# First norm of a streaming encoder layer: shared load buffers, small loads on GpSimd's queue, another order of the modulation steps

## The chip, the cores and the metric

The kernel runs on one core of a Trainium2 chip, as one program. The metric is the device time of a run in microseconds. The kernel before took 885.54, 887.25 and 888.99 us in three runs, median 887.25 us. TensorE is written PE, VectorE DVE, ScalarE ACT, GpSimd POOL and SyncE SP; SP issues nearly all of the DMAs here.

## The reference

One layer of a streaming encoder, 512 prompt tokens and 64 sample tokens, width 1024. Only its beginning matters for the change:

```python
def residual_block(x, c, mixer, w_ada, b_ada, norm1_g, w_out, norm2_g, w_ff1, w_ff2):
    sh1, sc1, g1, sh2, sc2, g2 = ada_modulation(c, w_ada, b_ada)   # silu(c) @ w_ada + b_ada, in six parts
    h = rms_norm(x, norm1_g) * (1 + sc1) + sh1
    ...
    # mixer(h): h @ w_in, split into q, k, v, qi, ki, wi, ga, gb;
    # sparse attention on the first six, a causal convolution on ga * sigmoid(gb);
    # then the output projection, a second modulated norm, a squared-ReLU MLP, a final norm
```

## The kernel before, in words

The two matrices `w_ada` and `w_in` come from HBM while the norm is computed, so the beginning is a race between loads and arithmetic. "The front" here means all up to the first matmul of the projection of `qi` (line L288), which starts 58.26 us into the profiled span. What follows it (projection, attention, convolution, MLP) is the same in both kernels.

- **Loads (L125 to L185).** SP issues them in program order: the conditioning rows `crow`, five token tiles `xtok0` to `xtok4` (L135) with six small loads into `rows` between them (biases and gains, L139), then `w_ada` in five blocks. A block (`BLOCKS`, `load_block`, L143 to L153) holds the shift and the scale columns for two (blocks 0 to 2) or one (blocks 3, 4) of the eight 128-wide slices of the width; it is four DMAs into tiles tagged `ada`, of which there are 10. Between the blocks come three slices of `w_in` (`load_w`): `ki`, `gb0`, `ga0`, and six small loads into `small` (convolution weights and state, L177 to L179). POOL's queue holds no DMA.
- **Constants (L189 to L207).** POOL makes the index matrix `jp`, `ones`, `onec`, `eps` and zeroes `cs`; DVE makes the identity from `jp`. ACT's first instruction that needs one of them reads `eps`.
- **Norm (L255 to L272).** For each token tile ACT squares and sums (L259), takes the root (L260), DVE scales, PE transposes against the identity (L270), ACT and DVE copy into `hat`. `columns` (L210) turns `crow` and `rows` and gives `cs` = silu(c) (L214).
- **Modulation step of a block (`mod_steps`, L225 to L249).** 16 matmuls on PE (L232, 32 rows in the trace: a plain f32 matmul shows two rows), ACT copies the result into `modrow`, PE turns it with `sel` (L239), DVE adds the biases and forms the scale (L246, L249).
- **Slices (`modulate`, L276).** For slice k, ACT writes the rounded high half of `h` (L281), DVE the full value (L282) and the low half (`sub`, L113).
- **Weights (`first_w`, L383).** ACT writes the high half of a weight slice, another engine the low half (L113): POOL for `ki` and `gb0`, DVE for `ga0`. They are called `fw0`, `fw1`, `fw2` in the trace's names, high and low half `fw00`, `fw01` and so on.
- **Products (`products(k, m, ...)`, L397).** For slice k and weight m, six matmuls at L406 of 288 columns each: high times high, low weight times high, high weight times low, for two halves of the tokens. There are 8 x 3 = 24 products, written (k, m) below, and they add up in six banks.

The orders of PE, ACT and DVE are written out by hand (the `manual_schedule` from L188, and the calls from `next(fr[0])` on to `step(...)`): what is called first is issued first on each of the three. In a `step`, a number b takes the next part of block b (first its matmuls, then the rest of the step with the first slice, then the second slice), and a tuple is products. POOL and SP take their instructions in the order of the program. An engine issues in order, so an instruction that waits holds up all that stand behind it.

Of the kernel before, what the change touches and what calls it, by code (L numbers as in the profile page):

```python
# [7 lines left out]
FT = mybir.dt.float32  # L8
# [7 lines left out]
D = 1024  # L16
# [13 lines left out]
TOPS = 256  # L30
FF = 4096
W = 31
ADA = 10
VEC, PEC = (0, 3), (1, 2)

P = dict(PRW=30, TPE=5, CS0=43, KYW=5, TAP=2, T0=20, IDX=2, TKS=12, ATT=4, SMP=6, MOD=21, CPW=15, MODL=6, S0=4, KEYW=5, TAPW=8, SCW=14, MODW=20, QIW=6, CSW=16, TKW=9, TK2=2, TKP=2, ATW=6, SMW=6, TT=3, CN1=8, CN2=21, CN3=8, RT=3, CNW=17)
HALO = W - 1
# [32 lines left out]
def step_kernel(ctx: ExitStack, tc: tile.TileContext, io):  # L70
    nc = tc.nc
    act, dve, pool, pe = nc.scalar, nc.vector, nc.gpsimd, nc.tensor

    def new_pool(stack, name, bufs=1):
        return stack.enter_context(tc.tile_pool(name=name, bufs=bufs, reuse_waits="tile"))
# [11 lines left out]
    def bank(tag, bufs):  # L87
        return ps.tile([128, 512], FT, name="ps_" + tag, tag=tag, bufs=bufs)

    def p_acc():  # L90
        return bank("acc", 3)

    def p_lg():
        return bank("lg", 2)

    def p_tp():
        return bank("tp", 2)

    def p_av():
        return bank("av", 1)  # L100
# [18 lines left out]
    def xtile(i):  # L119
        return (x_p[128 * i:128 * i + 128], 128) if i < 4 else (x_s, SAMP)  # L120

    start = ExitStack()
    stp = new_pool(start, "start")

    rows = stp.tile([128, 128], FT, name="rows")  # L125
# [5 lines left out]
    xt = []  # L131
    for i in range(5):
        src, n = xtile(i)
        t = stp.tile([128, D], FT, name=f"xtok{i}")
        nc.sync.dma_start(t[:n], src)  # L135
        xt.append((t, n))
        for r, ap in parts[2 * i:2 * i + 2]:
            k = ap.shape[1] // 128
            nc.sync.dma_start(rows[r:r + k, :], ap.rearrange("o (n c) -> (o n) c", c=128))  # L139

    BLOCKS = ((0, 2), (2, 2), (4, 2), (6, 1), (7, 1))

    def load_block(b):  # L143
        f0, nf = BLOCKS[b]
        tiles = []
        for v in range(2):
            for kh in range(2):
                t = stp.tile([128, 4, 256], FT, name="ada", tag="ada", bufs=ADA)[:, :, :128 * nf]
                c0 = 1024 * v + 128 * f0
                nc.sync.dma_start(t, w_ada[512 * kh:512 * kh + 512, c0:c0 + 128 * nf].rearrange("(k p) c -> p k c", p=128))  # L150
                tiles.append(t)
        return tiles
# [3 lines left out]
    def load_w(name, src, r0, c0, n=128):  # L156
        raw = wgt.tile([128, NK, 128], FT, name="wraw", tag="wraw", bufs=3)
        nc.sync.dma_start(raw[:, :, :n], src[r0:r0 + 1024, c0:c0 + n].rearrange("(k p) c -> p k c", p=128))
        wraw[name] = (raw, n)

    def split_w(name, hi=None, lo=None, eng=pool):
        raw, n = wraw.pop(name)
        if hi is None:
            hi = wgt.tile([128, NK, 128], FR, name="whi", tag="whi", bufs=2)
            lo = wgt.tile([128, NK, 128], FR, name="wlo", tag="wlo", bufs=2)
        copy_to(act, hi[:, :, :n], raw[:, :, :n])
        sub(eng, lo[:, :, :n], raw[:, :, :n], f(hi[:, :, :n]))
        return hi, lo, n

    small = stp.tile([128, 2, 512], FT, name="small")  # L170
    pool.memset(small[:, 0], 0.0)
    pool.memset(small[:64, 1], 0.0)
    ada = [load_block(0)]
    load_w("ki", w_in, 0, C_KI, 72)
    for s in range(4):
        n = 8 if s < 3 else 7
        nc.sync.dma_start(small[32 * s:32 * s + n, 0], io["conv_w"][0][s:s + 4 * n - 3:4])  # L177
    nc.sync.dma_start(small[:W, 1], io["conv_w"][0])
    nc.sync.dma_start(small[32:32 + HALO, 1], io["state_conv"][0, 0])  # L179
    load_w("gb0", w_in, 0, C_GB)  # L180
    ada.append(load_block(1))
    load_w("ga0", w_in, 0, C_GA)
    for b in (2, 3, 4):
        ada.append(load_block(b))


    begin = ExitStack()
# [3 lines left out]
    ones = cst.tile([128, 128], FT, name="ones")  # L191
# [117 lines left out]
    def fetch():  # L309
        if order:  # L310
            raw = wgt.tile([128, 1024], FT, name="wraw", tag="wraw", bufs=3)
            src = order.pop(0)
            nc.sync.dma_start(raw.rearrange("p (k c) -> p k c", k=src.shape[1]), src)
            raws.append(raw)

    def split():
        if raws:
            raw = raws.pop(0)
            hi = wgt.tile([128, 1024], FR, name="whi", tag="whi", bufs=2)
            lo = wgt.tile([128, 1024], FR, name="wlo", tag="wlo", bufs=2)  # L320
            for c in (slice(0, 512), slice(512, 1024)):
                copy_to(act, hi[:, c], raw[:, c])
                behind[0] = pool.tensor_tensor(lo[:, c], raw[:, c], f(hi[:, c]), op=OP.subtract).ins  # L323
            ready.append((hi, lo))
# [58 lines left out]
    def first_w(m, eng):  # L383
        hl = [stp.tile([128, NK, 128], FR, name=f"fw{m}{z}") for z in range(2)]
        fw[m] = split_w(("ki", "gb0", "ga0")[m], *hl, eng=eng)
# [11 lines left out]
    def products(k, *ms):  # L397
        h = hT[k]
        for i in ((0, 1), (2,)):
            for m in ms:  # L400
                hi, lo, n = fw[m]
                for j in range(2):
                    t = banks[2 * m + j][:n, :HALF]
                    for z in i:
                        w, x = ((hi, 0), (lo, 0), (hi, 1))[z]
                        pe.matmul(t, lhsT=w[:, k, :n], rhs=h[:, x, JS[j]], start=k + z == 0, stop=k == NK - 1 and z == 2)  # L406
# [36 lines left out]
    def step(*todo):  # L443
        if not banks:
            banks.extend([p_acc(), p_acc(), p_acc(), p_lg(), p_lg(), p_av()])
        for e in todo:
            if isinstance(e, int):
                next(fr[e])
            else:
                products(*e)  # L450

    next(fr[0])
    first_w(0, pool)
    next(fr[0])
    setup = conv_setup()
    next(setup)
    first_w(1, pool)
    step((0, 0), 0)
    next(setup, None)
    step((1, 0), (0, 1))  # L460
    first_w(2, dve)
    step(1, (1, 1), 1, 1, (0, 2), (1, 2), (2, 0, 1, 2), (3, 0))
    step(2, (3, 1), 2, 3, 2, (3, 2), 3, (4, 0, 1, 2))
    fetch()
    fetch()
    ckr = big.tile([128, 8, 2, 64], FT, name="ckr", tag="b")
    for s in range(2):
        nc.sync.dma_start(ckr[:, :, s, :], io["cache_kidx"][0, 0].rearrange("(n p) d -> p n d", p=128))
    step(4, (5, 0), 4)
    split()  # L470
    step((5, 1), (5, 2), (6, 0), (7, 0))
    for j in range(2):
        evac_ki(j, banks[j][:, :HALF], JS[j])
    step((6, 1), (7, 1), (6, 2), (7, 2))
# [898 lines left out]
```

## Time and profile before

| what | value |
|---|---|
| runs | 885.54, 887.25, 888.99 us |
| profiled execution | 887.81 us, its span 885.8 us |
| mean granted clock of PE | 0.963 of full speed |
| busy share of the span | PE 92%, DVE 58%, ACT 45%, POOL 33% |
| DMA | 95.55 MB, 107 GB/s of HBM over the span |
| first L288 matmul | 58.26 us into the span |

All times below are in microseconds from the span's start in the profiled execution. The page's row for PE reads `4898997977988999...` in 40 slices of some 22 us each: the first slice, 40% busy, and a part of the second and third are the front. The page's row for DMA reads `8984165...`: the first three slices are nearly full of transfers. The page's chain of waits covers the later part only, so the front is read from the timelines of the engines.

### The profile page before, as it was taken

To read this page: it belongs to the slowest core of one execution; us is meant where nothing else is said; L and a number is where in the kernel's file an instruction comes from. 1 tells how busy PE (TensorE), PEld (TensorE's weight loads), DVE (VectorE), ACT (ScalarE), POOL (GpSimd) and SP (SyncE) were. 2 spreads that over 40 slices of the span, in tenths; PEclk is the share of its full clock that TensorE was granted. 3 is DMA by queue.
4 is the path that set the end of the run, shared out by engine and by line. 5 is a ranking of instruction groups with operands and counts; after the bars stand their busy time and mean duration, and the time that the engine had idled before them with its cause. 6 is when DMAs were issued, how large, how long until landed. Compare 5 with 4: busy or idle time off the path is not lost. (4 is left out here: it accounts for less than half of the span.)

```text
span 885.8 us, 17048 instructions
## 1 busy us (share of the span) xinstructions
PE 815.4 (92%) x6787; PEld 758.7 (86%) x6787; DVE 509.6 (58%) x1133; ACT 402.0 (45%) x897; POOL 294.9 (33%) x273
## 2 busy tenths in 40 slices
PE   4898997977988999999899899998999989999996
PEld 3697894657877888989899899997999989999995
DVE  3579879999996344645856412663126631266343
ACT  5365554555876787554454211442124421244322
POOL 1155423122435323232423243332433333333700
PEclk9799998989999999999999899998999989999999
DMA  8984165445434356542312223222232223222411
GB/s 233 302 219 122 36 179 131 118 97 145 114 94 120 100 153 177 161 120 72 90 41 85 72 72 90 79 72 72 72 96 73 72 72 87 81 72 72 143 61 47
DMA packets 164553, 95.55 MB, mean 108 GB/s; under 512 B 7699, under 2 KB 161119, under 8 KB 164475
## 3 DMA queue, kind: packets, MB, share of 16 engines
q1 hardware_dynamic: 164475, 94.48, 38.3%
q8 instruction: 53, 0.87, 0.4%
q14 instruction: 25, 0.20, 0.1%
HBM read 88.82 MB, written 5.64 MB: 107 GB/s over the span
## 5 line engine op out<-in xcount | busy, mean ns | idle before, releaser
L113 POOL TENSOR_TENSOR wlo<-wraw,whi 128x1024 fp32r<-128x1024 f32 x52 | 125.0, 2403 | 239.0 <-ACT whi L104 230.0
L288 PE MATMUL ps_acc<-h,whi 128*128 128x288 f32 (+1 forms) x608 | 190.2, 313 | 0.0
L289 PE MATMUL ps_acc<-h,whi 128*128 128x288 f32 (+1 forms) x608 | 181.2, 298 | 0.0
L290 PE MATMUL ps_acc<-h,wlo 128*128 128x288 f32 (+1 forms) x608 | 180.8, 297 | 0.0
L104 ACT ACTIVATE whi<-wraw 128x512 fp32r<-128x512 f32 (+1 forms) x112 | 90.6, 823 | 151.4 <-PE ps_acc L289 49.0
L323 POOL TENSOR_TENSOR wlo<-wraw,whi 128x512 fp32r<-128x512 f32 x60 | 80.0, 1349 | 159.3 <-ACT whi L104 159.0
L288 PEld LDWEIGHTS ps_acc<-h,whi 128*128 128x128 f32 x608 | 115.9, 191 | 14.0 <-issue 12.7
L289 PEld LDWEIGHTS ps_acc<-h,whi 128*128 128x128 f32 x608 | 116.1, 191 | 0.9
L290 PEld LDWEIGHTS ps_acc<-h,wlo 128*128 128x128 f32 x608 | 116.0, 191 | 0.0
L1246 DVE TENSOR_TENSOR z<-z 128x288 f32<-128x288 f32 x64 | 79.3, 1242 | 43.4 <-ACT z L1245 43.4
L1078 DVE SCALAR_TENSOR_TENSOR x<-ps_acc,mod,x 128x288 f32<-128x288 f32 (+4 forms) x90 | 35.8, 422 | 95.5 <-PE ps_acc L290 95.3
L104 ACT ACTIVATE a<-z 128x288 fp32r<-128x288 f32 x64 | 28.2, 443 | 79.4 <-DVE z L1246 79.4
L555 DVE SCALAR_TENSOR_TENSOR yc<-u,cw,yc 128x606 f32<-128x606 f32 x60 | 58.6, 984 | 0.6
L1245 ACT ACTIVATE z<-z,bs 128x64 f32<-128x64 f32 (+2 forms) x96 | 39.9, 449 | 34.4 <-DVE z L1242 34.3
L113 DVE TENSOR_TENSOR a<-z,a 128x288 fp32r<-128x288 f32 x64 | 35.4, 556 | 29.7 <-ACT a L104 28.7
L738 ACT ACTIVATE gc<-sful,sg 128x544 bf16<-128x544 f32 x48 | 35.8, 746 | 32.1 <-DVE sg L736 31.3
L288 PE MATMUL ps_acc<-a,whi 128*128 128x288 f32 x168 | 49.9, 297 | 0.0
L290 PE MATMUL ps_acc<-a,wlo 128*128 128x288 f32 x168 | 49.9, 297 | 0.0
L289 PE MATMUL ps_acc<-a,whi 128*128 128x288 f32 x168 | 49.8, 297 | 0.0
L289 PE MATMUL ps_lg<-h,whi 128*128 128x290 f32 (+1 forms) x160 | 47.4, 296 | 0.0
L290 PE MATMUL ps_lg<-h,wlo 128*128 128x290 f32 (+1 forms) x160 | 47.3, 296 | 0.0
L288 PE MATMUL ps_lg<-h,whi 128*128 128x290 f32 (+1 forms) x160 | 47.2, 295 | 0.0
(359 smaller groups left out, 2110.1 us busy)
## 6 DMA issues: line engine op xcount, KB each, us to landing
wraw<-w_ff SPq DMA_DIRECT2D x64, 512.0 KB
ada<-w_ada SPq DMA_DIRECT2D x44, 512.0 KB
wraw<-w_in SPq DMA_DIRECT2D x24, 512.0 KB
wraw<-w_out SPq DMA_DIRECT2D x8, 512.0 KB
rep<-ud SPq DMA_DIRECT2D x24, 115.0 KB
xtok<-x_prompt SPq DMA_DIRECT2D x4, 512.0 KB
ada<-w_ada SPq DMA_DIRECT2D x8, 256.0 KB
ct<-cache_k SPq DMA_DIRECT2D x8, 256.0 KB
```

Of the source, the lines that this page charges most:

```text
L104: act.activation(out, in_, AF.Copy, scale=1.0 if scale is None else scale)
L113: eng.tensor_tensor(out, a, b, op=OP.subtract)
L288: pe.matmul(out, lhsT=hi, rhs=src[:, 0, cs_], start=first, stop=False)
L289: pe.matmul(out, lhsT=hi, rhs=src[:, 1, cs_], start=False, stop=False)
L290: pe.matmul(out, lhsT=lo, rhs=src[:, 0, cs_], start=False, stop=last)
L323: behind[0] = pool.tensor_tensor(lo[:, c], raw[:, c], f(hi[:, c]), op=OP.subtract).ins
L555: dve.scalar_tensor_tensor(yc[c], src, w, yc[c], op0=OP.mult, op1=OP.add)
L738: act.activation(eq, sful, AF.Sign, bias=cands[:, z:z + 1], scale=-1.0, accum_out=cnts[:, z:z + 1])
L1078: dve.scalar_tensor_tensor(xm[:, a:b], t[:, a - r.start:b - r.start], mod[:, g, s, m:m + 1], xm[:, a:b], op0=OP.mult, op1=OP.add)
L1245: act.activation(q, q, AF.Relu, bias=bs[:, s:s + 1])
L1246: dve.tensor_tensor(z[:, 1, r], z[:, 0, r], z[:, 0, r], op=OP.mult)
```

## The change

`ADA` goes from 10 to 15 and the five token tiles take their buffers under the same tag, so that later blocks may reuse a token tile's buffer. The six loads into `rows` and the six into `small` are issued by POOL instead of SP, the latter behind the loads of the blocks in program order. The low halves of `ki` and `gb0` are computed by DVE instead of POOL. A new function `warm(n)` issues n matmuls of `ones` by `ones` on PE whose result nobody reads. The order of modulation steps and products is another.

```diff
-ADA = 10
+ADA = 15
...
-        t = stp.tile([128, D], FT, name=f"xtok{i}")
+        t = stp.tile([128, D], FT, name=f"xtok{i}", tag="ada", bufs=ADA)
...
-            nc.sync.dma_start(rows[r:r + k, :], ap.rearrange("o (n c) -> (o n) c", c=128))
+            pool.dma_start(rows[r:r + k, :], ap.rearrange("o (n c) -> (o n) c", c=128))
...
-    for s in range(4):
-        n = 8 if s < 3 else 7
-        nc.sync.dma_start(small[32 * s:32 * s + n, 0], io["conv_w"][0][s:s + 4 * n - 3:4])
-    nc.sync.dma_start(small[:W, 1], io["conv_w"][0])
-    nc.sync.dma_start(small[32:32 + HALO, 1], io["state_conv"][0, 0])
     load_w("gb0", w_in, 0, C_GB)
     ada.append(load_block(1))
     load_w("ga0", w_in, 0, C_GA)
     for b in (2, 3, 4):
         ada.append(load_block(b))
+    for s in range(4):
+        n = 8 if s < 3 else 7
+        pool.dma_start(small[32 * s:32 * s + n, 0], io["conv_w"][0][s:s + 4 * n - 3:4])
+    pool.dma_start(small[:W, 1], io["conv_w"][0])
+    pool.dma_start(small[32:32 + HALO, 1], io["state_conv"][0, 0])
...
+    def warm(n):
+
+        t = p_tp()
+        for _ in range(n):
+            pe.matmul(t[:, :128], lhsT=ones, rhs=ones, start=True, stop=True)
+
+    first_w(0, dve)
+    warm(6)
     next(fr[0])
-    first_w(0, pool)
+    warm(3)
     next(fr[0])
     setup = conv_setup()
     next(setup)
-    first_w(1, pool)
+    first_w(1, dve)
     step((0, 0), 0)
     next(setup, None)
-    step((1, 0), (0, 1))
     first_w(2, dve)
-    step(1, (1, 1), 1, 1, (0, 2), (1, 2), (2, 0, 1, 2), (3, 0))
-    step(2, (3, 1), 2, 3, 2, (3, 2), 3, (4, 0, 1, 2))
+    step((0, 1, 2), 1, (1, 0), 1, 1, (1, 1, 2), (2, 0, 1, 2))
+    warm(8)
+    step(2, (3, 0), 2, 2, (3, 1, 2), (4, 0), 3, (4, 1), 3, (4, 2), (5, 0, 1), 4)
...
-    step(4, (5, 0), 4)
+    step((5, 2), 4, (6, 0), (7, 0))
     split()
-    step((5, 1), (5, 2), (6, 0), (7, 0))
```

What moves on POOL. Before, its queue begins (behind a few constants of the runtime) with the two memsets of `small` and then the constants:

```order
L171 MEMSET small 128x512
L172 MEMSET small 64x512
L195 ISA
L195 IOTA jp 128x128
L202 MEMSET ones 128x128
L203 MEMSET onec 128x128
L204 MEMSET eps 128x1
```

Now the six loads into `rows` stand at the start of the queue (the last of them is the first row here), and the six into `small` between the memsets and the constants:

```order
L139 DMA rows<-conv_ln_b 4x128
L171 MEMSET small 128x512
L172 MEMSET small 64x512
L182 DMA small<-conv_w 8x512 x3
L182 DMA small<-conv_w 7x512
L183 DMA small<-conv_w 31x512
L184 DMA small<-state_conv 30x512
L195 ISA
L195 IOTA jp 128x128
L202 MEMSET ones 128x128
L203 MEMSET onec 128x128
L204 MEMSET eps 128x1
```

So twelve DMA issues stand ahead of `jp`, `ones` and `eps`, on which DVE's identity, PE's transposes and ACT's first square wait.

What moves on PE ahead of block 1's modulation step, the first L232 row in each piece. Before, the product (0, 1) stands there, with weights `fw10` and `fw11` (`gb0`), behind the last matmul of (1, 0); `h_305` is slice 0 and `h_398` slice 1:

```order
L406 MATMUL ps_acc_387<-h_398,fw00_295 72x288
L406 MATMUL ps_acc_388<-h_305,fw10_382 128x288
L406 MATMUL ps_acc_388<-h_305,fw11_383 128x288
L406 MATMUL ps_lg_389<-h_305,fw10_382 128x288
L406 MATMUL ps_lg_389<-h_305,fw11_383 128x288
L406 MATMUL ps_acc_388<-h_305,fw10_382 128x288
L406 MATMUL ps_lg_389<-h_305,fw10_382 128x288
L232 MATMUL ps_tp_427<-ada_117,cs_169 32x256
```

Now (0, 1) and (0, 2) stand there, with `fw10`, `fw11` (`gb0`) and `fw20`, `fw21` (`ga0`); slice 0 is `h_316`:

```order
L406 MATMUL ps_acc_399<-h_316,fw11_394 128x288
L406 MATMUL ps_lg_400<-h_316,fw10_393 128x288
L406 MATMUL ps_lg_400<-h_316,fw11_394 128x288
L406 MATMUL ps_lg_401<-h_316,fw20_422 128x288
L406 MATMUL ps_lg_401<-h_316,fw21_423 128x288
L406 MATMUL ps_av_402<-h_316,fw20_422 128x288
L406 MATMUL ps_av_402<-h_316,fw21_423 128x288
L406 MATMUL ps_acc_399<-h_316,fw10_393 128x288
L406 MATMUL ps_lg_400<-h_316,fw10_393 128x288
L406 MATMUL ps_lg_401<-h_316,fw20_422 128x288
L406 MATMUL ps_av_402<-h_316,fw20_422 128x288
L232 MATMUL ps_tp_438<-ada_111,cs_169 32x256
```

Block 1's step now stands behind products that need the low half of `ga0` (`fw21`), seven matmuls of them from the first use of `fw21` on; before it did not. In both kernels 21 of the 24 products come behind that step.

What moves on PE at the end of the modulation. Before, three products of ready slices, (5, 1), (5, 2) and (6, 0), stand between the last L239 and the first product of slice 7; the first seven matmuls of them:

```order
L239 MATMUL ps_tp_640<-sel_173,modrow_632 128x4
L406 MATMUL ps_acc_388<-h_565,fw10_382 128x288
L406 MATMUL ps_acc_388<-h_565,fw11_383 128x288
L406 MATMUL ps_lg_389<-h_565,fw10_382 128x288
L406 MATMUL ps_lg_389<-h_565,fw11_383 128x288
L406 MATMUL ps_acc_388<-h_565,fw10_382 128x288
L406 MATMUL ps_lg_389<-h_565,fw10_382 128x288
L406 MATMUL ps_lg_390<-h_565,fw20_423 128x288
```

Now only (6, 0) stands there, six matmuls of slice 6 (`h_615`), and then slice 7 (`h_677`):

```order
L239 MATMUL ps_tp_672<-sel_173,modrow_657 128x4
L406 MATMUL ps_acc_397<-h_615,fw00_276 72x288
L406 MATMUL ps_acc_397<-h_615,fw01_277 72x288
L406 MATMUL ps_acc_398<-h_615,fw00_276 72x288
L406 MATMUL ps_acc_398<-h_615,fw01_277 72x288
L406 MATMUL ps_acc_397<-h_615,fw00_276 72x288
L406 MATMUL ps_acc_398<-h_615,fw00_276 72x288
L406 MATMUL ps_acc_397<-h_677,fw00_276 72x288
L406 MATMUL ps_acc_397<-h_677,fw01_277 72x288
```

Two products fewer stand between the last L239 and slice 7.

## Rows read from the trace of the kernel before

**Rows 1.** Windows: busy us (count) of PE, PEld, DVE, ACT, POOL; clock, DMA, GB/s.

```profile
35.70:58.25 22.55, 22.55 (x238) 20.73 (x235) 12.29 (x35) 12.44 (x25) 4.01 (x4) 1.00 0.82 213
24.60:35.70 11.10, 8.75 (x119) 5.79 (x107) 6.63 (x10) 4.56 (x9) 2.44 (x1) 0.54 1.10 341
```

**Rows 2.** Timeline of PE: start, length, line, operation, count, [idle before <-releaser].

```profile
16.64 0.41 PE L270 MATMUL ps_lg<-ident,xtok 64*128 64x64 f32 x4
...
20.05 1.91 PE L232 MATMUL ps_tp<-ada,cs 128*32 128x256 f32 x26 [1.38 <-DMA ada<-w_ada]
22.44 0.61 PE L239 MATMUL ps_tp<-sel,modrow 128*128 128x4 f32 x4 [0.47 <-ACT modrow L104]
...
30.36 1.60 PE L406 MATMUL ps_acc<-h,fw 128*72 128x288 f32 x6 [2.24 <-issue]
...
32.85 2.92 PE L232 MATMUL ps_tp<-ada,cs 128*32 128x256 f32 x32
...
41.98 1.93 PE L232 MATMUL ps_tp<-ada,cs 128*32 128x256 f32 x32
...
58.26 0.29 PE L288 MATMUL ps_acc<-h,whi 128*128 128x288 f32 x1
```

**Rows 3.** Timeline of POOL: the constant `eps`, and the low half of `gb0`.

```profile
2.23 0.23 POOL L204 MEMSET eps<- 128x1 f32 x1
...
26.68 2.44 POOL L113 TENSOR_TENSOR fw<-wraw,fw 128x1024 fp32r<-128x1024 f32 x1 [2.22 <-ACT fw L104]
```

**Rows 4.** Lines L139 and L177 on SP: DMA issues, ns min/median/max.

```profile
L139 SPq DMA_DIRECT2D rows<-b_ada x1: 425/425/425, 1.9 to 1.9; - x1
...
L177 SPq DMA_DIRECT2D small<-conv_w x4: 288/296/1751, 13.9 to 16.4; - x4
```

**Rows 5.** Timeline of ACT: squares of the first tiles, `cs`, the high half of `ga0`.

```profile
5.24 1.06 ACT L259 ACTIVATE junk<-xtok 128x1024 bf16<-128x1024 f32 x1 [2.54 <-DMA xtok<-x_prompt]
...
7.47 1.06 ACT L259 ACTIVATE junk<-xtok 128x1024 bf16<-128x1024 f32 x1 [0.76 <-DMA xtok<-x_prompt]
...
12.00 1.06 ACT L259 ACTIVATE junk<-xtok 128x1024 bf16<-128x1024 f32 x1 [0.30 <-DMA xtok<-x_prompt]
...
17.11 0.25 ACT L214 ACTIVATE cs<-ps_tp 128x8 f32<-128x8 f32 x2
...
33.26 1.06 ACT L104 ACTIVATE fw<-wraw 128x1024 fp32r<-128x1024 f32 x1 [5.15 <-DMA wraw<-w_in]
```

**Rows 6.** Timeline of PE: two groups of four transposes, 128 columns each.

```profile
12.26 0.65 PE L270 MATMUL ps_acc<-ident,xtok 128*128 128x128 f32 x4 [0.71 <-DVE xtok L262]
12.75 0.60 PE L270 MATMUL ps_lg<-ident,xtok 128*128 128x128 f32 x4
```

**Rows 7.** Timeline of DVE: scales, slices, low halves.

```profile
23.36 1.12 DVE L249 SCALAR_TENSOR_TENSOR mod<-mod,cols 128x4 f32<-128x4 f32 x1
24.51 0.77 DVE L282 TENSOR_SCALAR hfull<-hat,mod 128x512 f32<-128x512 f32 x2
...
26.36 2.81 DVE L282 TENSOR_SCALAR hfull<-hat,mod 128x512 f32<-128x512 f32 x2
...
29.95 0.18 DVE L428 TENSOR_TENSOR i<-ident 128x32 f32<-128x32 f32 x1
...
34.35 1.22 DVE L113 TENSOR_TENSOR fw<-wraw,fw 128x1024 fp32r<-128x1024 f32 x1 [3.77 <-ACT fw L104]
...
37.40 0.16 DVE L249 SCALAR_TENSOR_TENSOR mod<-mod,cols 128x4 f32<-128x4 f32 x1
...
53.68 0.76 DVE L113 TENSOR_TENSOR h<-hfull,h 128x576 fp32r<-128x576 f32 x1 [0.41 <-ACT h L281]
```

**Rows 8.** Windows ahead of `gb0` and behind it; the last column is GB/s.

```profile
18.00:22.00 4.00, 2.59 (x30) 1.03 (x28) 0.00 (x0) 0.12 (x1) 0.00 (x0) 1.00 0.65 136
24.00:36.00 12.00, 9.65 (x180) 6.69 (x181) 7.19 (x11) 4.68 (x10) 2.89 (x2) 0.57 1.10 340
```

**Rows 9.** Timeline of PE: the last turn of a modulation row.

```profile
51.72 0.28 PE L239 MATMUL ps_tp<-sel,modrow 128*128 128x4 f32 x2
```

## The prediction, made before the changed kernel had run

> **What bounds the kernel now.** I read the windows first, then PE's timeline, then that of whichever engine PE waits for. In the windows the reader sees two stretches [rows 1]: from 35.70 on PE is busy for all of 22.55 us at full clock until the first L288 matmul at 58.26 [rows 2], and in the 11 us before that it is busy for 8.75 us at a mean clock of 0.54. So behind 35.70 nothing but PE's own work sets the time; ahead of it loads and other engines do. PE's timeline shows what it lacks there [rows 2]: block 0's columns (1.38 us of waiting), the low half of `gb0` and of slice 0 (2.24 us, put down to "issue"), and half the clock, at which the 32 rows of block 1's step take 2.92 us against 1.93 at full clock. That step ends at 35.70, and 21 products come behind it. In the changed kernel 21 products come behind it too. The forecast is therefore two questions: when does block 1's step end, and what is added behind it. All that comes after the front is the same, so I pass the shift on to the end one to one.
>
> The profiled execution took 887.81 us, 0.56 above the median of the runs. I sum against 887.81.
>
> **The constants behind twelve issues on POOL.** Before, `eps` is there at 2.46 [rows 3] and ACT starts squaring when the first token tile lands, at 5.24 [rows 5], so the constants have 2.8 us of cover. From there to the end of `cs` (17.36) are 12.1 us, of which 1.85 are three waits for tiles (0.76 the first, 0.30 the last) [rows 5]: 10.3 us of work. Now twelve DMA issues stand ahead of `jp`, `ones` and `eps`, at d us each; behind them wait DVE's identity, PE's transposes and ACT's first root, that is the whole norm. No DMA issue on POOL is in this trace. Bounds from the nearest rows: SP issues loads of the same tensors in 0.30 us (median) and one in 1.75 [rows 4]. With 0.30 the twelve take 3.6 us and nothing happens; with 1.75 they take 21. The ends are a factor of six apart; I take their middle as a ratio, 0.75 (nearer to the row of 0.425 for `b_ada` than to that of 1.75), and keep both. Then `eps` comes at 2.46 + 9.0 = 11.5, all tiles have landed by the time ACT wants them, and `cs` is ready at 11.7 + 10.3 = 22.0. Before, block 0's columns were the last to arrive (the wait at 20.05), so of the 4.6 us that `cs` is late 2.7 go into that wait.
>
> The Trainium skill ("DMA: Bandwidth & Descriptors", Specifications) gives DMAs of GpSimd's path a first byte after about 1 us and those of SP's path one after about 0.6 us. Scaling 0.30 by that ratio would make an issue 0.5 us and the twelve 6 us, an estimate by that page under which the issues stay hidden; taken as it stands, 1 us each, it gives 12 us and the dear case below. No row here shows which, and my sum uses neither.
>
> **Block 0's step, with idle matmuls in front.** In [rows 6] the second group of four transposes starts 0.49 us behind the first, 0.12 a row; a plain f32 matmul shows two rows, so one of `warm` costs 0.24. The six of `warm(6)` take 1.4 us behind the last transposes, which end 0.3 us before `cs` does (16.64 + 0.41 against 17.36) [rows 2, 5]: block 0's matmuls start at 22.0 - 0.3 + 1.4 = 23.1 and end 1.93 later, at 25.1 (before: 21.96). From there to the finished scale it took 2.5 us before, 1.12 of them in a DVE instruction that elsewhere takes 0.16 [rows 7]; it ran beside POOL's low half of `ki`, which DVE now does itself earlier, so 1.5 us remain. `warm(3)`, 0.7 us, replaces a wait of 0.47 for ACT's copy [rows 2]: +0.25. The scale is ready at 26.9 (before 24.48).
>
> **DVE's longer list up to the low half of `ga0`.** From the scale on, DVE now does: slice 0's full value and, 1.2 us after the scale, its low half (0.76), the low half of `gb0` (1.22), slice 1's full value (0.77) and low half (0.76), three small additions (0.18 each), the low half of `ga0` (1.22) [rows 7]; with 0.2 us for ACT's high halves that is 6.7 us. The gain in it is real: POOL needed 2.44 us for what DVE does in 1.22 and held DVE's next instruction at 2.81 instead of 0.77 [rows 3, 7]. But `fw21` is ready at 26.9 + 6.7 = 33.6, and PE now wants it before block 1's step.
>
> **The loads.** SP's queue loses twelve issues and the stream its gap: between 18 and 22 it moved 136 GB/s, afterwards 340 [rows 8], so 4 x (1 - 136/340) = 2.4 us are to be had. `ga0` then lands at 33.26 - 2.4 = 30.9 instead of 33.26 [rows 5], and `fw21` follows 2.3 us behind the start of its high half (33.26 to 34.35 + 1.22), at 33.2. That floor holds whatever POOL does; POOL decides once d is over 0.72. The extra buffers let blocks 2 to 4 load earlier, which removes no wait: behind 35.70 PE had none.
>
> **End of block 1's step.** Behind `fw21` PE still has seven matmuls of (0, 1) and (0, 2) and the 32 rows. Both ran at half clock here before, and PE waits no less now, so I take half: 2.85 us for the rows as in [rows 2], 0.24 each for the matmuls (PE's six at 30.36 are 1.60 us). 33.6 + 1.7 + 2.85 = 38.1, against 35.70: **+2.4**.
>
> **Behind it.** `warm(8)` adds 8 x 0.24 = 1.9 us; block 2's columns have landed by then, so it hides in no wait: **+1.9**. At the end, slice 7's low half was ready 2.4 us after the last L239 ended and its high half 1.6 us after (L239 until 52.0, the low half from 53.68 to 54.44) [rows 7, 9]. Before, three products of 0.8 us each (six matmuls at 0.133) lay between; now one does: a stall of 0.8 for the high half, then two thirds of a product, then 0.3 for the low: **+1.1**. The same happens to (4, 0), which has two products ahead of it and misses the low half by 0.4: **+0.4**. Slice 4 to 6 and block 4 have more cover. The other reorderings leave PE the same work.
>
> Sum: 2.4 + 1.9 + 1.1 + 0.4 = **+5.8**: 887.81 + 5.8 = 893.6 on the profiled execution, 893.0 against the median. I predict 893.2.
>
> **Rivals.**
> - *Dear issues.* Each further 0.1 us of d moves everything up to block 1's step by 1.2. At d = 1.0: +3.0 on the forecast, 896.4; at 1.25: 899.4; at the bound of 1.75, 905. For it: nothing else stands between POOL and the norm. Against: the median issue of 0.30 on SP.
> - *Cheap issues and full clock.* With d under 0.7 the floor of 33.2 decides, and if the idle matmuls keep PE's clock at full, seven matmuls and 32 rows take 0.9 + 1.93: 36.1, +0.4. With 3.4 behind it: +3.8, 891.3; with a stream another 1 us earlier, 890.3. For it: full clock in all of [rows 1]'s first stretch, where PE has no gap. Against: PE has a wait in front of `fw21` that the idle matmuls don't fill.
> - *Not slower: the early stream.* Without the small loads SP's queue is free of twelve issues at 0.30 (3.6 us) while the tiles load, so tiles and block 0 land early and ACT's three waits go: `cs` at 5.24 + 10.3 = 15.5, block 0's step ends by 18.6, the scale is ready at 20.4, block 0 lands at 20.0 - 2.4 = 17.6 and `ki`, `gb0`, block 1 and `ga0` follow (six DMAs of 512 KB and one of 288, 3.4 MB, 10 us at 340 GB/s), `ga0` at 27.6, `fw21` at 29.9, block 1's step at full clock ends at 32.7: -3.0. With the 3.4 behind it that is +0.4, 887.6; if PE has to wait for block 2 anyway, which hides `warm(8)`, 885.7; if the stalls go too, 884.3. It decides if d is under 0.25 or so and the stream never falls below 340. For it: the gap in [rows 8] is real. Against: it needs all of that at once.
> - *The order changes nothing*: PE does (0, 2) early at the price of a wait it had anyway. That is the forecast without the stalls (-1.5): 891.7, inside the forecast's range.
>
> **How the numbers follow.** A measurement of this kernel tells about 0.5% (4.4 us) from no change, so "slower" begins at 891.7 and "faster" ends at 882.8. Chances: forecast (891.5 to 894.5) 0.40, nearly all of it slower; dear issues 0.25, all slower; cheap issues at full clock 0.17, nearly all within 0.5%; early stream 0.18, of which I give 0.10 to faster, for a sum in which the parts behind the step are hidden and the stream beats 340, and 0.08 to no change. Slower 0.25 + 0.36 = 0.61, same 0.04 + 0.17 + 0.08 = 0.29, faster 0.10. For 8 in 10 the range leaves out the early stream's faster half and the dearest issues (d over 1.25): 885.5 to 899.5.
>
> **What would show it.** On POOL's timeline `eps` should start at about 11 us (2.23 + 12 d), and ACT's first square right behind it with no wait for a tile. PE's timeline should show a wait in (0, 2) for DVE's `fw`, 32 rows of block 1's step ending near 38, eight pairs of `ones` rows before block 2's step with no wait behind them, and a gap ahead of the first matmuls of slice 7. The first L288 matmul should start near 64. I am wrong if ACT's first square still starts near 5, if block 1's step ends before 35.7, or if the first L288 matmul comes before 62.7 although `eps` is late.

## The result, and the profile after

In sixteen runs each, the changed kernel took 893.78 us (median; 891.55 to 897.49) and the kernel before 888.14 (885.54 to 892.81). The ratio is 1.0061, its 95% interval 1.0044 to 1.0078: slower by 0.6%, 3.9 to 6.9 us. The forecast was 893.2, slower. The time is right; of the terms of its sum some are, and some came out right only together. Of the runs further down, one execution of early_setup (1101.93 us, at a mean clock of 0.65) counts in that kernel's median and not in its ratio.

The profiled execution of the changed kernel took 891.55 us (span 889.8), which is the fastest of its sixteen. On POOL's timeline (start, length, line, operation, count) the reader sees the first of the twelve issues and, behind the last, `eps`:

```profile
1.27 0.72 POOL L139 DMA_DIRECT2D rows<-b_ada  x1 [0.82 <-POOLq L1366]
1.98 1.04 POOL L139 DMA_DIRECT2D rows<-norm_g  x2
...
9.77 0.26 POOL L204 MEMSET eps<- 128x1 f32 x1
```

The twelve add up to 6.3 us, 0.525 each (0.50 to 0.72), not 0.75. `eps` starts at 9.77 instead of 2.23 [rows 3]; of the 1.2 us that the issues don't account for, 0.7 are two pauses between the loads into `small` (0.36 us put down to an earlier load, 0.34 to "issue"). The Trainium skill ("DMA: Bandwidth & Descriptors", Specifications) gives a first byte after about 1 us on GpSimd's path and about 0.6 us on SP's, from which the prediction had an estimate of 0.5 an issue. These rows lie close to that estimate, which doesn't show that the first byte is what an issue costs.

ACT's timeline: the first square without a wait for a tile, `cs`, and the high half of `ga0`, which still waits for its load.

```profile
10.18 1.04 ACT L259 ACTIVATE junk<-xtok 128x1024 bf16<-128x1024 f32 x1
...
20.28 0.25 ACT L214 ACTIVATE cs<-ps_tp 128x8 f32<-128x8 f32 x2
...
30.21 1.06 ACT L104 ACTIVATE fw<-wraw 128x1024 fp32r<-128x1024 f32 x1 [1.10 <-DMA wraw<-w_in]
```

The norm is 4.9 us later than in [rows 5] (10.18 against 5.24), `cs` 3.2 us, and `ga0` 3.05 us earlier (30.21 against 33.26). PE's timeline of the front, to be laid beside [rows 2, 9]:

```profile
21.85 1.93 PE L232 MATMUL ps_tp<-ada,cs 128*32 128x256 f32 x32
...
28.46 0.33 PE L422 MATMUL ps_lg<-ident,small 128*32 128x8 f32 x10 [1.98 <-issue]
...
32.58 0.40 PE L406 MATMUL ps_lg<-h,fw 128*128 128x288 f32 x1 [0.67 <-DVE fw L113]
...
33.70 1.93 PE L232 MATMUL ps_tp<-ada,cs 128*32 128x256 f32 x32
...
40.87 1.95 PE L456 MATMUL ps_tp<-ones 128*128 128x128 f32 x16
...
48.45 0.49 PE L406 MATMUL ps_acc<-h,fw 128*72 128x288 f32 x2 [0.29 <-DVE h L113]
...
57.05 0.82 PE L406 MATMUL ps_acc<-h,fw 128*72 128x288 f32 x4 [0.53 <-ACT h L281]
58.17 0.74 PE L406 MATMUL ps_acc<-h,fw 128*72 128x288 f32 x4 [0.31 <-DVE h L113]
...
61.66 0.30 PE L288 MATMUL ps_acc<-h,whi 128*128 128x288 f32 x1
```

Block 1's step ends at 35.64, where it ended before (35.76), but not by the same way: it starts 0.85 us later (33.70 against 32.85) and runs at full clock, 1.93 us for 2.92. From its end to the first L288 matmul it is 26.0 us instead of 22.5. Those 3.5 us are in the rows: 1.9 for `warm(8)`, waits of 0.29 in (4, 0), 0.53 and 0.31 in (7, 0). Each wait costs some 0.16 more than it shows, because matmuls that follow each other overlap (0.29 long, 0.13 apart). The first L288 matmul is 3.40 us later than before, and the shift is passed on: the copy into `mix` on ACT that starts at 286.27 in the trace before starts at 290.00 here (+3.73), and the profiled executions differ by 3.74.

```profile
286.27 0.28 ACT L104 ACTIVATE mix<-ps_av 128x128 fp32r<-128x128 f32 x1 [0.30 <-PE ps_av L878]
```

```profile
290.00 0.28 ACT L104 ACTIVATE mix<-ps_av 128x128 fp32r<-128x128 f32 x1 [0.29 <-PE ps_av L885]
```

(The first row is of before, the second of after.) The medians differ by 5.6. One thing that may set the profiled execution apart from the median is its clock. Windows of after, columns as in [rows 1]:

```profile
30.00:32.00 2.00, 1.91 (x7) 1.34 (x5) 1.58 (x5) 1.06 (x1) 0.00 (x0) 0.56 1.10 350
32.00:34.00 2.00, 1.42 (x15) 1.17 (x19) 0.52 (x1) 0.00 (x0) 0.00 (x0) 1.00 1.09 348
```

It is back at full by 32 us, and block 1's step takes 1.93 us. I therefore traced the changed kernel a second time.

### The profile page after: what moved, and what is told of

Same layout as the page of the kernel before. It is cut to its first block, busy times and chain, and to the rows that moved or that the text cites. A ratio compares the mean times of both kernels' runs of the same rounds, so it can differ in the third digit from the quotient of the medians.

```text
span 889.8 us, 17128 instructions
## 1 busy us (share of the span) xinstructions
PE 817.4 (92%) x6821; PEld 762.3 (86%) x6821; DVE 508.9 (57%) x1135; ACT 401.7 (45%) x897; POOL 297.4 (33%) x283
## 5 line engine op out<-in xcount | busy, mean ns | idle before, releaser
L288 PE MATMUL ps_acc<-h,whi 128*128 128x288 f32 (+1 forms) x608 | 190.3, 313 | 0.0
L288 PEld LDWEIGHTS ps_acc<-h,whi 128*128 128x128 f32 x608 | 115.9, 191 | 14.0 <-issue 12.4
L288 PE MATMUL ps_acc<-a,whi 128*128 128x288 f32 x168 | 50.0, 297 | 0.0
L288 PE MATMUL ps_lg<-h,whi 128*128 128x290 f32 (+1 forms) x160 | 47.2, 295 | 0.0
```

The source lines that it names most:

```text
L288: pe.matmul(out, lhsT=hi, rhs=src[:, 0, cs_], start=first, stop=False)
```

## The experiments

Each ratio below is to runs of the kernel before that were taken beside that kernel (medians 887.8 to 889.3 us); a difference from the changed kernel's median, 893.78 us, is between runs that were not taken side by side. "The step" is block 1's step.

### The changed kernel once more (after_again)

The edit: none.

> The changed kernel once more, unchanged, for a second trace. Its first one was the fastest of sixteen executions, and block 1's step ran at full clock in it (33.70 to 35.64); in the runs no_warm8 and tail_cover, which are the same kernel up to that step, it ran at half (35.1 to 37.6 and 38.0). Theory H (half is the rule, and the median of the sixteen holds it): block 1's step ends at 37 to 38.5 here and the first L288 matmul comes at 63 to 64.5. Rival (full is the rule, the two others differ by their code): 35.5 to 35.8 and 61.5 to 62.

One execution, 897.76 us (before beside it: 887.06). PE's timeline and two windows:

```profile
34.88 3.63 PE L232 MATMUL ps_tp<-ada,cs 128*32 128x256 f32 x32
...
64.53 0.30 PE L288 MATMUL ps_acc<-h,whi 128*128 128x288 f32 x1
```

```profile
32.00:34.00 2.00, 1.35 (x5) 1.10 (x5) 0.84 (x1) 0.00 (x0) 0.00 (x0) 0.50 1.09 349
34.00:36.00 2.00, 2.00 (x16) 1.19 (x19) 0.00 (x0) 0.00 (x0) 0.00 (x0) 0.50 1.16 316
```

Theory H held, at the upper edge of its ranges: at half clock the step ends at 38.51, 2.87 us later than in the first trace of the same program, and again 26.0 us stand behind it. Up to 28 us the two traces agree within 0.3 us. So the front costs +3.4 us at full clock and +6.3 at half. But the half clock's share isn't passed on whole. The copy into `mix`, which starts at 290.00 in the first trace, starts here at

```profile
291.21 0.27 ACT L104 ACTIVATE mix<-ps_av 128x128 fp32r<-128x128 f32 x1
```

and of the 2.87 us 1.2 are left. The rest of the 6.2 us between the two executions arises behind that, the largest part in one stretch where PE is as busy and the clock differs (windows of after, then of after_again):

```profile
448.00:454.00 6.00, 6.00 (x49) 5.97 (x48) 0.32 (x2) 1.70 (x2) 0.58 (x1) 1.00 0.01 2
```

```profile
448.00:454.00 6.00, 6.00 (x35) 6.00 (x35) 0.00 (x0) 0.00 (x0) 0.00 (x0) 0.72 0.11 31
```

The measured 5.6 lies between the two traces; how much of it is the clock of the front, these two don't settle.

### Without the eight idle matmuls (no_warm8)

```diff
-    warm(8)
```

> The changed kernel without the eight idle matmuls ahead of block 2's step. Theory A (the loss of 3.4 us in the front lies behind block 1's step: 1.9 for these matmuls, the rest in stalls): the first L288 matmul moves from 61.66 to 59.8, the time falls by 1.9 us. Theory C (the idle matmuls pay for themselves by the clock): the granted clock falls below 1.00 somewhere between 41 and 50 us and the first L288 matmul stays at 61 or later.

892.86 us, ratio to before 1.0050 [1.0023, 1.0077]; 0.9 us under the changed kernel's median, inside the uncertainty. The trace:

```profile
35.07 2.52 PE L232 MATMUL ps_tp<-ada,cs 128*32 128x256 f32 x32
...
61.80 0.30 PE L288 MATMUL ps_acc<-h,whi 128*128 128x288 f32 x1
```

The first L288 matmul comes at 61.80 and not at 59.8, which alone would speak for theory C. But the step ahead of the missing matmuls ends at 37.59 here (half clock for most of it); from its end on it takes 24.2 instead of 26.0 us, at full clock. So A's 1.8 us is there, and no clock pays it back. The forecast compared whole times, and the noise ahead of the edit was as large as its effect.

### Idle matmuls around block 0's step removed (no_warm63)

```diff
-    warm(6)
     next(fr[0])
-    warm(3)
```

> The changed kernel without the six and the three idle matmuls around block 0's step. Theory A: block 0's step starts about 1.4 us earlier, everything up to the low half of ga0 is ready earlier but ga0 (30.2) is not, so the first L288 matmul stays within 0.4 us of 61.66 if the clock stays. Theory C: the clock of PE is half when block 1's step runs, which then takes 2.9 instead of 1.93, and the first L288 matmul comes 1 us or more later.

894.33 us, 1.0063 [1.0035, 1.0090], as the changed kernel. In the trace the step ran at half clock and ended at 38.46, with the first L288 matmul at 64.61, so its trace agrees with theory C. But the changed kernel itself did the same in its second trace (38.51, 64.53): in these traces the nine matmuls cost nothing that can be seen, and the full clock doesn't follow from them.

```profile
30.39 0.61 PE L406 MATMUL ps_lg<-h,fw 128*128 128x288 f32 x1 [2.00 <-issue]
...
34.81 3.64 PE L232 MATMUL ps_tp<-ada,cs 128*32 128x256 f32 x32
```

### The constants ahead of POOL's issues (consts_first)

The edit, shortened:

```diff
+    pool.iota(jp, ...); pool.memset(ones, 1.0); pool.memset(onec, 1.0 / 512.0); pool.memset(eps, EPS); pool.memset(cs, 0.0)
     rows = stp.tile([128, 128], FT, name="rows")
...
-    (the same five further down)
```

> The changed kernel with jp, ones, onec, eps and cs made by POOL ahead of its twelve DMA issues. Theory A: ACT's first square goes from 10.2 back to about 5.7 and cs from 20.5 to about 16, but ga0 lands at 30.2 as before, its low half is ready at 32.5 as before and the first L288 matmul stays within 0.4 us of 61.66. Theory P (the late norm is what the change costs): all behind moves earlier by most of the 2 us by which block 0's step was late, the first L288 matmul at 59.5 to 60.

896.55 us, 1.0090 [1.0061, 1.0120]: 2.8 us above the changed kernel's median, with overlapping intervals, though the norm is early. ACT, then PE:

```profile
5.19 1.06 ACT L259 ACTIVATE junk<-xtok 128x1024 bf16<-128x1024 f32 x1 [2.95 <-DMA xtok<-x_prompt]
```

```profile
28.27 0.38 PE L422 MATMUL ps_lg<-ident,small 128*32 128x8 f32 x10 [5.17 <-issue]
...
34.63 3.10 PE L232 MATMUL ps_tp<-ada,cs 128*32 128x256 f32 x32
...
63.69 0.30 PE L288 MATMUL ps_acc<-h,whi 128*128 128x288 f32 x1
```

Theory P falls: the norm starts 5 us earlier and block 1's step ends at 37.74 all the same (`ga0` still lands at 30.3, for which ACT waits). PE spends what it gained in a wait of 5.17 us "for issue", which ends at 28.27; in after the same wait lasts 1.98 and ends at 28.46. In all the traces so far this wait stands ahead of the 219th or 220th matmul row of the program, whichever line that is: in the convolution setup in after, in (0, 1) in no_warm63, in (1, 0) in before and old_order. That is a place in the instruction stream, not in the data. The trace of before alone shows as much: its row 219 is the third matmul of (1, 0), which takes the high halves of `ki` and of slice 1. ACT had written the latter by 27.63, 2.7 us before the row starts at 30.36, and the low half of `gb0` is first used five rows further on.

```profile
26.50 1.13 ACT L281 ACTIVATE h<-hat,mod 128x512 fp32r<-128x512 f32 x2
```

### The kernel before with nine idle matmuls (before_warm)

```diff
+    warm(6)
     next(fr[0])
     first_w(0, pool)
+    warm(3)
     next(fr[0])
```

> The kernel before with nine idle matmuls (18 rows on PE), six ahead of block 0's step, where PE waits for loads anyway, and three behind it. Theory I (PE's unexplained wait of 2.24 us is for its own next instructions: it stands ahead of the 219th matmul row in all traces so far and ends 1.2 to 1.5 us after a 16 KB transfer on the instruction queue): the wait stands 18 rows earlier in the kernel's work, inside L422, the transfer starts near 26 instead of 27.85 and the wait ends near 28.5 instead of 30.36; the first L288 matmul comes 0.5 to 1.5 us earlier, 56.8 to 57.8. Rival D (PE waits there for the low halves that POOL and DVE write): the wait ends at 30.0 to 30.5 ahead of the same matmul of product (0, 0) and the first L288 matmul stays at 58.0 to 58.6.

```profile
28.47 0.33 PE L422 MATMUL ps_lg<-ident,small 128*32 128x8 f32 x10 [4.18 <-issue]
...
32.52 1.93 PE L232 MATMUL ps_tp<-ada,cs 128*32 128x256 f32 x32
...
56.91 0.29 PE L288 MATMUL ps_acc<-h,whi 128*128 128x288 f32 x1
```

Theory I held: the wait moved 18 rows up in the work, to L422, and ended at 28.47 instead of 30.36. The view of the DMA queues shows one transfer on the instruction queue between 20 and 30 us in both kernels; it lies between 27.5 and 29.5 before, and between 25.5 and 27.5 here (before, then before_warm):

```profile
q8 instruction: 1, 0.02, 3.6%
```

```profile
q8 instruction: 1, 0.02, 3.1%
```

That PE waits for its own instructions is the reading that fits these rows; none of them says whose instructions the transfer carries. Nor does each such transfer cost PE something: in before the next one lies between 34 and 36, beside as dense a stream of loads (348 GB/s), and PE is busy all the time:

```profile
q8 instruction: 1, 0.02, 3.6%
```

```profile
34.00:36.00 2.00, 2.00 (x26) 0.94 (x19) 1.22 (x1) 0.34 (x2) 0.00 (x0) 0.78 1.08 348
```

The first L288 matmul came 1.35 us earlier, and yet the time is the same: 888.43 us, 0.9994 [0.9977, 1.0011]. The 1.35 us and 1.25 more were lost in the attention near 100 us, where PE waited 3.0 us for ACT instead of 1.6, at half the clock; 1.15 came back by 204 us (windows of before, then of before_warm):

```profile
98.00:104.00 6.00, 5.44 (x36) 5.05 (x37) 4.76 (x9) 4.55 (x11) 0.00 (x0) 1.00 0.02 5
```

```profile
98.00:104.00 6.00, 6.00 (x26) 5.55 (x25) 3.01 (x6) 2.46 (x6) 0.00 (x0) 0.56 0.02 5
```

### The order of before with the new loads (old_order)

The edit puts the hand-written order of before back and drops the idle matmuls; loads, buffers and DVE's low halves stay new.

> The changed kernel's loads, buffers and DVE low halves, with the hand-written order of the kernel before and no idle matmuls. Theory A: block 1's step no longer waits for ga0; block 1 lands at 28.4 and the step ends at 33.5 to 34.7 (clock full or half) instead of 35.70 before, with 22.55 us of work behind it: first L288 matmul at 56 to 57.5, 1 to 2 us faster than before. Rival (loads and low halves are worth nothing in this order either): first L288 matmul at 58.0 to 58.6, the time of before.

889.57 us, 1.0018 [0.9996, 1.0040]: no change from before that can be told.

```profile
30.39 1.47 PE L406 MATMUL ps_acc<-h,fw 128*72 128x288 f32 x5 [1.72 <-issue]
...
32.75 2.91 PE L232 MATMUL ps_tp<-ada,cs 128*32 128x256 f32 x32
...
58.15 0.29 PE L288 MATMUL ps_acc<-h,whi 128*128 128x288 f32 x1
```

My forecast of 56 to 57.5 failed, and the rival held: although `ga0` lands 2.9 us earlier (30.39 for 33.26) and the low half of `gb0` is done 0.8 us earlier (28.3 for 29.1), PE's wait "for issue" ends at 30.39 as before (30.36), and all behind it is as before. The interval doesn't overlap the changed kernel's [1.0044, 1.0078], so the slowdown of the change is in its order and its idle matmuls; its loads and low halves are worth nothing where that wait decides.

### Block 1's step ahead of (0, 2) (mod1_first)

```diff
-    step((0, 1, 2), 1, (1, 0), 1, 1, (1, 1, 2), (2, 0, 1, 2))
+    step((0, 1), 1, (0, 2), (1, 0), 1, 1, (1, 1, 2), (2, 0, 1, 2))
```

> The changed kernel with block 1's step ahead of product (0,2), so that it no longer waits for the low half of ga0. Theory A (that wait and the work in front cost what I booked): block 1's step starts at 31 to 32 and ends at 33.5 to 35 (it ended at 35.6 and 37.6 in the two traces so far), 0.8 us more stands behind it, and the first L288 matmul comes at 60 to 61.8, 1 to 2 us ahead of the changed kernel. Rival: PE then waits for ga0 behind the step just as long; the first L288 matmul within 0.4 us of 61.7 to 63.6.

891.78 us, 1.0044 [1.0022, 1.0065]: 2.0 us under the changed kernel's median, with overlapping intervals.

```profile
31.95 1.93 PE L232 MATMUL ps_tp<-ada,cs 128*32 128x256 f32 x32
...
60.73 0.30 PE L288 MATMUL ps_acc<-h,whi 128*128 128x288 f32 x1
```

Theory A held in the main: the step no longer waits for `fw21`, ends at 33.9, at full clock, and 26.8 us stand behind it. Beside the changed kernel's trace at full clock (35.64, 61.66) the first L288 matmul comes 0.9 us earlier, a little less than the 1 to 2 us expected.

### Cover ahead of slice 7 (tail_cover)

```diff
-    step((5, 2), 4, (6, 0), (7, 0))
+    step((5, 2), 4, (6, 0), (6, 1), (6, 2), (7, 0))
```

> The changed kernel with (6,1) and (6,2) ahead of (7,0) instead of behind it, all else the same. Theory A: the two waits in (7,0), 0.53 and 0.31 us, go, and from the end of block 1's step to the first L288 matmul it takes 24.9 to 25.2 us instead of 26.0; 1 us faster than the changed kernel. Rival: the waits only move to (7,1), 26.0 stays. Up to block 1's step it is the changed kernel word for word: if the full clock in that step (it ended at 35.64 in the profiled execution, the fastest of sixteen) was an exception, it ends at 37 to 38.5 here; if it is the rule, at 35.5 to 35.8.

```profile
35.05 2.96 PE L232 MATMUL ps_tp<-ada,cs 128*32 128x256 f32 x32
...
63.50 0.37 PE L288 MATMUL ps_acc<-h,whi 128*128 128x288 f32 x1 [0.75 <-DVE kip L113]
```

The waits in (7, 0) went, as theory A said, but 0.75 us of them came back ahead of L288, where PE now waits for DVE's evacuation of `ki`: 25.5 us behind the step, half of the gain expected. The time, 894.14 us, 1.0054 [1.0033, 1.0075], can't tell half a microsecond. The step ended at 38.0, for the most part at half clock again.

### The setup in the wait for block 0 (early_setup, early_mod1, early_mod1_warm)

If PE's wait for instructions decides, the 132 rows of the convolution setup belong where PE is idle anyway: ahead of block 0's step. Constants first, no idle matmuls (the edit, shortened, with lines joined):

```diff
+    setup = conv_setup(); next(setup); next(setup, None)
     first_w(0, dve); next(fr[0]); next(fr[0]); first_w(1, dve)
-    setup = conv_setup(); next(setup); step((0, 0), 0); next(setup, None); ...
+    step((0, 0), 0, (0, 1), (1, 0)); first_w(2, dve)
+    step(1, (1, 1), 1, 1, (0, 2), (1, 2), ...)   # from here on the order of before
```

> The changed kernel's loads, buffers and DVE low halves, the constants ahead of POOL's DMA issues, no idle matmuls, the convolution setup moved ahead of block 0's step (where PE waits for loads), then the products (0,0), (0,1), (1,0), and the order of before from block 1's step on. Theory I: the setup's 132 rows go through PE before 19 us, so the next instructions are asked for earlier and the wait ahead of row 219 is gone or over before block 1 lands at 28.4; block 1's step ends at 30.4 to 31.4 and the first L288 matmul comes at 53.5 to 56, a time of 883 to 885.5. Rival: the instruction transfer still comes at 26 to 28 and the clock is half, block 1's step ends at 34 or later and the first L288 matmul stays at 57 or later, no gain on the kernel before.

886.03 us, 0.9966 [0.9950, 0.9983]: faster than the kernel before by 0.3%, and by the two ratios than the changed one by 0.9%.

```profile
30.11 3.08 PE L232 MATMUL ps_tp<-ada,cs 128*32 128x256 f32 x32
...
55.64 0.29 PE L288 MATMUL ps_acc<-h,whi 128*128 128x288 f32 x1
```

No wait is left ahead of row 219, and the transfer on the instruction queue that lay between 27.5 and 29.5 in before lies between 20.5 and 22 here:

```profile
q8 instruction: 1, 0.02, 5.0%
```

The step ends at 33.2 and not at 30.4 to 31.4, since it ran at half clock and (1, 0) held PE until 30.1; the time is a little above the range expected. No run moves the setup alone, without the early constants and the new loads, so the 0.3% belongs to all of them together. Two variants:

> early_setup with product (1,0) behind block 1's step instead of in front of it: PE is then free when block 1's columns land (28.9 in early_setup, where the step started at 30.1). Theory A (block 1's step ends the front, 22.5 us stand behind it): the step starts at 28.5 to 29, ends at 30.5 (full clock) to 32 (half), 0.8 us more stands behind it, first L288 matmul at 54 to 55.5; up to 1.5 us faster than early_setup. Rival: PE waits behind the step for the low half of ga0 (32.9 in early_setup) what it wins in front, first L288 matmul at 55.4 to 56.

> The kernel of the run early_mod1 with four idle matmuls ahead of the convolution setup and four behind block 0's step, both where PE waits for other engines. Theory C (a wait of PE costs twice, once by itself and once by the half clock behind it, and idle matmuls save the second part where they stand in a wait): the clock stays at 1.00 in block 0's step, which takes 2 us instead of 4.2 with its wait, and block 1's step takes 1.93 instead of 3.1; first L288 matmul 1 us or more ahead of early_mod1's. Rival: the clock falls all the same or the eight matmuls cost 2 us by themselves; first L288 matmul at the same time as early_mod1's or later.

The first gave 886.81 us, 0.9977 [0.9955, 0.9999], the second 886.93, 0.9981 [0.9958, 1.0003]. PE of the first, then of the second:

```profile
27.52 3.61 PE L232 MATMUL ps_tp<-ada,cs 128*32 128x256 f32 x32
...
54.33 0.29 PE L288 MATMUL ps_acc<-h,whi 128*128 128x288 f32 x1
```

```profile
28.51 1.91 PE L232 MATMUL ps_tp<-ada,cs 128*32 128x256 f32 x26 [0.99 <-DMA ada<-w_ada]
...
53.70 0.29 PE L288 MATMUL ps_acc<-h,whi 128*128 128x288 f32 x1
```

In the traces, each of which is the fastest of its kernel's twelve executions, the first L288 matmul comes 3.9 and 4.6 us ahead of the kernel before; the second holds full clock from 16 us on and gains 0.6, not the 1 us that theory C wanted. In the second, PE stands for 1.00 us ahead of row 219 again, until 22.66, but behind it PE has to wait for the low half of `gb0` until 25.57 anyway. In the timings the three can't be told apart.

## Why the prediction was right

*The prediction's own signs.* It was to be wrong if the step ended before 35.7, or if the first L288 matmul came before 62.7 although `eps` is late. In the profiled execution both happened (35.64 and 61.66, with `eps` at 9.77), in the second trace neither (38.51 and 64.53). That the median of 893.78 lies so close to 893.2 is therefore in part luck: the sum holds an end of the step that one trace of four doesn't show, and a shift passed on one to one that held for the first trace (+3.73 at 290 us) and not for the second, nor for before_warm.

*The constants behind POOL's issues.* Right that they become late (11 us forecast, 9.77 measured), wrong in size, 0.525 us an issue for 0.75 (0.63 with the pauses), and wrong in weight. I wrote that POOL decides "once d is over 0.72"; below that the floor of the loads should decide, and consts_first shows that removing the delay altogether moves block 1's step by nothing (37.74 against 37.59 to 38.51 in the three traces in which it ran at half clock for the most part).

*DVE's list and the loads.* `fw21` was to be ready at 33.6, with a floor of 33.2 from the loads. It was ready at 32.5, 2.3 us behind `ga0` (30.21), as the floor was built; `ga0` gained 3.05 us for 2.4. PE did wait for it, 0.67 us, as said, and mod1_first shows that this place in the order costs, 0.9 us between the two traces at full clock.

*The end of block 1's step.* Forecast 38.1 at half clock, "+2.4". In the first trace it was 35.64, at full clock, in the second 38.51 and in the two other kernels with the same front 37.59 and 38.01. So the term was right for three of four traces, with two errors under it that cancel: `fw21` came 1.1 us earlier (0.75 in the second trace), and the seven matmuls and the 32 rows took 1.98 and 3.63 us at half clock instead of 1.7 and 2.85 (the row of 2.92 in [rows 2] ends at full clock). The step that failed is the reading of PE's wait. The prediction named the low half of `gb0` and of slice 0 as what PE lacked for 2.24 us ("put down to 'issue'"); before_warm and old_order show that the wait stands at a place in PE's instruction stream and that no faster load or low half shortens it; that it is for PE's own instructions is the likeliest reading, not shown directly.

*Behind the step.* Forecast +1.9, +1.1 and +0.4, together 3.4; measured 3.5 in both traces, with 1.9, 1.2 (0.53 and 0.31, and 0.32 for the lost overlap) and 0.45. This is the part that stands in every trace of this front, and the main cause of the slowdown that the runs show. It rests on the traces: the timings of no_warm8 and tail_cover are too coarse to show its pieces one by one.

*The rivals.* Dear issues did not come. "Cheap issues and full clock" gave 891.3, with +0.4 for the step and 3.4 behind it; the first trace (891.55, -0.1 and 3.5) is that case, the median is not. The early stream did bring `ga0` by 3 us, and in old_order the front gained nothing from it.

What stays open: how often the step runs at half clock. Of four traces with this front (after, after_again, no_warm8, tail_cover) one ran at full; later stretches vary by as much, so the share of each in the median isn't settled. Why full clock came back at 32 us in one and at 38 in another wasn't tried.

## What to carry to other kernels

A wait that the profile puts down to "issue" is worth a count of the instructions ahead of it: if it stays at the same count when the work around it moves, no faster producer helps, and instructions that are moved into an earlier idle stretch may (here early_setup, which moved the constants too). Work added behind the last wait of a saturated engine (idle matmuls, an order with less cover) is paid in full, while a gain ahead of it may end in the next wait. Where two executions of one program differ by more than an edit is worth, compare stretches of the traces at equal clock, not whole times, and look again further on before a shift is passed on to the end.

## What the hardware showed that I had not expected

- PE's wait ahead of matmul row 219 or 220 (with as many weight loads, some 440 instructions): 1.72 to 5.17 us in ten traces of ten that don't move the setup forward, ended at 28.3 to 28.9 us with nine idle matmuls ahead and at 30.4 without, always 1.2 to 1.5 us behind the end of the 16 KB transfer. The Trainium skill ("Runtime: NRT & Kernel Launch", Instruction fetch mechanics) says that instructions come in blocks of 16 KiB and that the cost of crossing a boundary is mostly hidden. The rows agree on the blocks (one transfer of 0.02 MB on the instruction queue just ahead of the wait's end), and on "mostly": the next transfer in before costs PE nothing, the first one 2.24 us. Both lie beside a load stream of some 340 GB/s, so the stream alone isn't what makes the first dear. What sets the time of that transfer was not tried.
- The clock: two executions of one program, alike up to 28 us, differ by 2.87 us at 64 us: after the same waits of PE full clock came back by 32 us in one and not before 38 in the other.
- POOL issued a small load in 0.50 to 0.55 us where SP took 0.30 (median), and that of `b_ada` in 0.72 where SP took 0.425 [rows 4].
